# A decoder layer on one core: fourteen gate/up tiles of the first feed-forward half put in pairs with seven block products for eight

## The chip, the cores and the metric

The program runs on one core of one Trainium2 chip. The time is that of one execution on the device in microseconds (us), as a median of several runs. A separate execution is recorded by the hardware profiler, and every duration of a single instruction comes from that one. The engines are PE (TensorE, matrix products; its weight loads are listed as PEld), DVE (VectorE), ACT (ScalarE), POOL (GpSimd) and SP (SyncE, which only issues transfers here).

## What is computed

One layer on 512 tokens of width 1024: a gated feed-forward half, a mixing part (dilated attention and a diagonal state model side by side), and a second gated feed-forward half.

```python
x = x + 0.5 * rms_norm(swiglu(rms_norm(x, ffn1_pre_g), ffn1_w_in, ffn1_w_out), ffn1_post_g)
h = rms_norm(x, mix_pre_g)
q, k, v, u = split(h @ w_mix_in)
a = dilated_attention(q, k, v)
s = s5_mixer(u, a_re, a_im, log_dt, b_re, b_im, c_re, c_im, d_skip, w_glu, b_glu)
x = x + rms_norm(concat([a, s]) @ w_mix_out, mix_post_g)
x = x + 0.5 * rms_norm(swiglu(rms_norm(x, ffn2_pre_g), ffn2_w_in, ffn2_w_out), ffn2_post_g)

def swiglu(x, w_in, w_out):          # w_in: 1024 x 5632, w_out: 2816 x 1024
    gate, up = split(x @ w_in)
    return (silu(gate) * up) @ w_out
```

All is float32. The change is in the first `swiglu`, and in the point of time at which `s5_mixer`'s parameters (powers of the state factor, the matrices that go in and out of the states) are worked out.

## The kernel before, in words

**Precision.** Each float32 factor is cut in a high part in the type fp32r (ACT, a cast) and a low part (the difference, on DVE or POOL). A product is three matmuls: high x high, high x low, low x high (`mm3`). `load` fetches a weight block to a `wraw` buffer (3 of them) and cuts it to `whi` and `wlo` (4 of each); its argument `pool` puts the subtraction on POOL, otherwise it is on DVE.

**Layout.** Activations stand with features on the 128 partitions and the 512 tokens along the free dimension. Big buffers of 8 x 512 columns come from one pool of six (`b16`): `x`, `xh`, `xl`, `y`, `ah`, `al` in the first half.

**First half, `ffn` (L371).** The 2816 hidden features are 22 tiles of 128. For each tile f, `products(f)` (L388) makes gate and up, each 8 blocks x 3 matmuls of 512 columns; `hidden(f)` (L396) scales by the norm factor `r`, takes silu(gate) x up and cuts the result to `ah`, `al`, in a ring of 8 slots. Output products (`outp`, L404) are made in three parts, each over all 8 output blocks m: over tiles 0 to 6 after tile 7, over 7 to 13 after tile 14, and over 14 to 17 after tile 21 (`FMAIN`). The first writes `y`, the others add to it. The last four tiles (18 to 21) are left to `boundary` (L261), which multiplies them with the tail weights `tw` in two halves of tokens, so that the norm behind them can begin early; `load_tail` fetches those weights during tiles 18 to 21.

**The state model's parameters, `ssm_params` (L726).** A generator that `ffn` resumes between matmuls (`hook`, `step`); 35 resumptions run it to its end. In order: loads; exponentials and sines of columns of 16 on DVE; powers `pw`; four pairs of complex products (128 x 256, DVE) whose results ACT copies to two large zeroed tiles `gb`; eight groups of transposes `w1t` on PE, each copied by ACT and written to memory (`w1d`); products `kb` in two parts and transposes `kc` on PE, with `kd` written; four more complex products, copied by ACT to `zb` (two tiles in the place of `gb`, zeroed by POOL) and written as `w2d`. All its tiles lie in pools that are closed when it has ended (`early`).

The steps stand at blocks k = 5 of each gate product and k = 1 and 5 of each up product from tile 2's up product on (L385).

**Second half, `swiglu_half` (L455).** Tiles 0 to 5 are made as in the first half. Tiles 6 to 21 are made in pairs, `pair` (L550). The 1024 input features are cut in two halves and the 512 tokens in two halves, gate and up are the two rows of blocks of the weights: a 2 x 2 by 2 x 2 product, which takes seven block products of weight sums with input sums in place of eight (the scheme of Strassen and Winograd). `sums` (L514) makes the sums of the inputs, scaled by gain and norm factor, once; `plain` (L530) cuts the four plain blocks; a pair makes its own sums of weights. A block product (`times`, L554) is 24 matmuls of 256 columns: two tiles x 4 blocks x 3.

**What sets the order.** A planner places the instructions on each engine by the program's order as priority and by readiness in its own model of time; those passed through `fix`, matmuls among them, keep the program's order. Each engine then works off its list in that fixed order, and the transfers issued by SP are one list too. Buffers of a ring are reused when their last reader has ended; a pool opened in the place of a closed one waits for the last use of what lay there.

Of the kernel before, what the change touches and what calls it, by code (L numbers as in the profile page):

```python
# [8 lines left out]
F32 = mybir.dt.float32  # L9
F32R = mybir.dt.float32r  # L10
I32 = mybir.dt.int32
AF = mybir.ActivationFunctionType
# [5 lines left out]
P = 128  # L18
S = 512
# [4 lines left out]
FMAIN = ((0, 7), (7, 7), (14, 4))  # L24
# [4 lines left out]
NSTD = 6  # L29
# [14 lines left out]
class Layer:  # L44
# [326 lines left out]
    def ffn(self, n, first, scope):  # L371
# [13 lines left out]
        other = ({5: step}, {1: step, 5: step})  # L385
        between = {(nfirst, 0): {}, (nfirst, 1): {6: lambda: late[0](fixp=self.fix)}, (nfirst + 1, 0): {6: late[1]}}

        def products(f):  # L388
            o[f] = []
            for i, c in enumerate((f, NF + f)):  # L390
                w = self.ahead.pop(0) if self.ahead else self.load(w_in[c], (KD, P), pool=i == 1)
                b = self.bank("gu")
                self.mmk(b, w, self.xh, self.xl, hooks=between.get((f, i), other[i]))
                o[f].append(b)
# [9 lines left out]
        def outp(i):  # L404
            f0, nf = FMAIN[i]
            for m in range(KD):
                wh, wl = self.load(w_out[m][:, f0:f0 + nf, :].rearrange("p k m -> p (k m)"), (nf, P), pool=m % 2 == 1)
                b = self.bank("yo")
                for k in range(nf):
                    s = (f0 + k) % RING  # L410
                    self.mm3(b, wh[:, k], wl[:, k], ah(s), al(s), k == 0, k == nf - 1)
                if i == 0:
                    nc.scalar.copy(out=y(m), in_=b)
                else:
                    nc.vector.tensor_tensor(out=y(m), in0=b, in1=y(m), op=ALU.add)

        for f in range(NF):
            if f >= nfirst:
                products(f)
            if f == lag:  # L420
                for i in range(lag):
                    hidden(i)
            if f >= lag:
                hidden(f)
            if f in (7, 14):
                outp(f // 7 - 1)
            if f == NF - NT:
                for _ in hook:
                    pass
                early.close()  # L430
                tp = scope.enter_context(self.tc.tile_pool(name="bd" + n, bufs=1))
            if f >= NF - NT:
                self.load_tail(tp, w_tail, f - (NF - NT), f % 2 == 1)
        tail = lambda k: (ah((NF - NT + k) % RING), al((NF - NT + k) % RING))
        outp(2)
# [19 lines left out]
    def swiglu_half(self, first, scope):  # L455
# [4 lines left out]
        nc, V, fx = self.nc, self.nc.vector, self.fix  # L460
# [43 lines left out]
        def wsum():  # L504
            return fin.tile([P, 1024], F32, name="wsum", tag="wsum", bufs=3)

        tq = [[fin.tile([P, 1024], F32R, name="tq", tag=f"tq{q}{i}") for i in range(2)] for q in range(3)]

        def quarter(t, i, j):
            return t.pair(slice(4 * i, 4 * i + 4))[:, :, j * HT:(j + 1) * HT]  # L510

        v4 = lambda t: t.rearrange("p (k c) -> p k c", c=HT)

        def sums():  # L514
            for k in range(KD):
                V.scalar_tensor_tensor(out=self.x(k), in0=self.x(k), scalar=self.g(4, k), in1=r, op0=ALU.mult, op1=ALU.mult)
            b = lambda i, j: quarter(self.x, i, j)
            n1, n2 = wsum(), wsum()
            V.tensor_tensor(out=v4(n1), in0=b(0, 0), in1=b(0, 1), op=ALU.subtract)
            V.scalar_tensor_tensor(out=v4(n2), in0=v4(n1), scalar=-1.0, in1=b(1, 1), op0=ALU.mult, op1=ALU.subtract)  # L520
            self.split(*tq[0], n2)
            t = wsum()
            V.scalar_tensor_tensor(out=v4(t), in0=v4(n2), scalar=-1.0, in1=b(1, 0), op0=ALU.mult, op1=ALU.subtract)
            self.split(*tq[2], t)
            t = wsum()
            V.tensor_tensor(out=v4(t), in0=b(1, 1), in1=b(0, 1), op=ALU.subtract)
            self.split(*tq[1], t)
            return n1

        def plain(n1):  # L530
            bh, bl = self.b16("bh", F32R), self.b16("bl", F32R)
            v = lambda t, q: t.rearrange("p (q k) c -> p q (k c)", q=4)[:, q]
            src = [quarter(self.x, 0, 0), quarter(self.x, 1, 0), quarter(self.x, 1, 1), v4(n1)]
            for q, s in enumerate(src):
                self.split(v4(v(bh, q)), v4(v(bl, q)), s)
            return [(v(bh, q), v(bl, q)) for q in range(4)]

        def block(f, up, kh, extra):
            t = (fin.tile([P, 1024], F32, name="wx", tag="wx", bufs=3) if extra else
                 self.wp.tile([P, 1024], F32, name="wraw", tag="wraw", bufs=3))  # L540
            src = w_in[f + NF * up:f + NF * up + 2, :, kh * S:(kh + 1) * S].rearrange("f p c -> p f c")
            nc.sync.dma_start(out=t.rearrange("p (f c) -> p f c", f=2), in_=src)
            return t

        def cut(t, pool=False):
            hi, lo = (self.wp.tile([P, 1024], F32R, name=n, tag=n, bufs=4) for n in ("whi", "wlo"))
            self.wsplit(t, hi, lo, pool)
            return hi, lo

        def pair(f, b11, b21, b22, n1, n2, t3, t4):  # L550
            add = lambda x, z, t: V.tensor_tensor(out=t, in0=x, in1=z, op=ALU.add)
            X = self.bank("wx")

            def times(bank, w, xb, first):  # L554
                for g in range(2):
                    for k in range(4):
                        c, m = slice(k * HT, (k + 1) * HT), slice((4 * g + k) * P, (4 * g + k + 1) * P)
                        st = first and g == 0 and k == 0
                        for i, (wi, xi) in enumerate(((0, 0), (0, 1), (1, 0))):
                            self.mm(bank[:, g * HT:(g + 1) * HT], lhsT=w[wi][:, m], rhs=xb[xi][:, c],  # L560
                                    start=st and i == 0, stop=g == 1 and k == 3 and i == 2, skip_group_check=True)

            def keep(bank):
                t = self.tmp("kp")
                nc.scalar.copy(out=t, in_=bank)
                return t

            p2 = lambda t: t.rearrange("p (f c) -> p f c", f=2)
            gt = fin.tile([P, 2, S], F32, name="gp", tag="gp", bufs=2)
            half = lambda t, h: t[:, :, h * HT:(h + 1) * HT]  # L570
            a11 = block(f, 0, 0, False)
            h11 = cut(a11)
            times(X, h11, b11, True)
            s1 = keep(X)
            a12 = block(f, 0, 1, False)
            h12 = cut(a12, True)
            Y = self.bank("wy")
            times(Y, h12, b21, True)
            V.tensor_tensor(out=half(gt, 0), in0=p2(Y), in1=p2(s1), op=ALU.add)
            a21, a22 = block(f, 1, 0, True), block(f, 1, 1, True)  # L580
            c3 = wsum()
            add(a11, a21, c3)
            c2 = wsum()
            add(c3, a22, c2)
            times(X, cut(c2), n2, False)
            s2 = keep(X)
            c1 = wsum()
            add(a21, a22, c1)
            Q = self.bank("wq")
            times(Q, cut(c1), n1, True)  # L590
            q = keep(Q)
            times(X, cut(c3), t3, False)
            V.tensor_tensor(out=q, in0=X, in1=q, op=ALU.add)
            add(c2, a12, c2)
            times(Q, cut(c2), b22, False)
            V.tensor_tensor(out=half(gt, 1), in0=p2(Q), in1=p2(s2), op=ALU.add)
            nc.scalar.activation(out=gt, in_=gt, func=AF.Silu)
            times(X, cut(a22, True), t4, False)
            s = f % RING
            dst = lambda t, h: half(t.pair(slice(s, s + 2)), h)  # L600
            for h, u in ((1, q), (0, X)):
                V.scalar_tensor_tensor(out=half(gt, h), in0=p2(u), scalar=-1.0, in1=half(gt, h), op0=ALU.mult, op1=ALU.mult)
                if f == NF - 2:
                    self.split(dst(ah, h), dst(al, h), half(gt, h))
            if f < NF - 2:
                self.split(ah.pair(slice(s, s + 2)), al.pair(slice(s, s + 2)), gt)

        for f in range(NSTD):
# [7 lines left out]
            if f == 3:  # L616
                for _ in hook:
                    pass
                n1 = sums()
        blocks = plain(n1)  # L620
# [3 lines left out]
        for f in range(NSTD, NF, 2):  # L624
            pair(f, *blocks, *tq)
            if f in (10, 16):
                outp(f // 6)
# [781 lines left out]
```

## Time and profile before

| | us |
|---|---|
| median of 3 runs | 941.23 |
| lowest and highest | 939.71 and 943.09 |
| the profiled execution | 939.08 |
| its span, first to last instruction | 937.3 |
| first half: tile 0 to the end of the third output product | 8.9 to 353.8 |
| second half: start of the first output product to the end of the last pair | 649.9 to 908.1 |

A row of the chain of waits or of the timeline gives start, length, engine or what, the line of the code, what is written and read, and the count (x24). L132 is the helper through which every matmul goes, so there the tile's name tells them apart: `gu` is a gate or up product, `yo` an output product, `yt` the tail's, `wx`, `wy`, `wq` the block products of a pair. A group's row ends with busy time, mean ns of one, and the idle time before with what ended it. A row of a view by stretches gives, for each engine, busy us and in brackets the number of instructions. "before" in square brackets means that the engine stood idle for that long.

### The profile page before, as it was taken

How to read it: one execution, taken by the hardware profiler on the slowest of the kernel's cores; microseconds unless marked ns; L12 is line 12 of the kernel's file. 1: busy time of each engine (PE TensorE's matmuls, PEld its weight loads, DVE VectorE, ACT ScalarE, POOL GpSimd, SP SyncE). 2: the span in 40 equal slices, each digit the busy share in tenths (PEclk: the TensorE clock that was granted, in tenths of full speed). 3: DMA queues.
4: the chain of work that ended last, by engine and by line, in shares of the span. 5: the costliest groups of instructions: out<-in, count | busy, mean ns of one | idle time of the engine just before them, and what ended most of it. 6: DMA issues, size and time to landing. Idle time of an engine off the chain costs nothing.

```text
span 937.3 us, 14181 instructions
## 1 busy us (share of the span) xinstructions
PE 925.7 (99%) x5658; PEld 803.6 (86%) x5658; DVE 588.5 (63%) x994; ACT 407.3 (43%) x650; POOL 225.0 (24%) x134
## 2 busy tenths in 40 slices
PE   8999999999999999999999999999999999999996
PEld 6888888888888889978777889988899989998995
DVE  6999214464246544947989467679357547745856
ACT  7354324452233322526637564465255414541542
POOL 0234222232223222420000024521222212221321
PEclk9999999999999999999999999999999999999999
DMA  8223333353334232086221452243323322332222
GB/s 272 90 93 118 105 106 124 131 180 101 113 107 144 75 123 69 24 236 174 87 83 57 136 180 92 75 150 113 113 91 111 116 90 90 113 113 91 92 90 90
DMA packets 44001, 106.74 MB, mean 114 GB/s; under 512 B 7808, under 2 KB 11136, under 8 KB 43392
## 3 DMA queue, kind: packets, MB, share of 16 engines
q1 hardware_dynamic: 42352, 102.21, 33.4%
q10 hardware_dynamic: 1584, 3.63, 1.1%
q8 instruction: 44, 0.72, 0.3%
q14 instruction: 21, 0.17, 0.1%
HBM read 96.13 MB, written 9.70 MB: 113 GB/s over the span
## 4 chain that ended last, share of the span: by engine, by line
PE 94%; DVE 3%; ACT 1%; issue 1%; DMA 0%; SPq 0%; POOLq 0%; POOL 0%; DVEq 0%; ACTq 0%
PE gu L132 29%; PE yo L132 21%; PE wx L132 10%; PE yt L132 6%; PE first L132 6%; PE wq L132 5%; PE prj L132 4%; PE wy L132 2%; PE prv L132 2%; PE mo L132 2%; PE st L132 1%; PE ys L132 1%; PE gl L132 1%; PE pt L999 1%; PE sc L132 1%
## 5 line engine op out<-in xcount | busy, mean ns | idle before, releaser
L107 POOL TENSOR_TENSOR wlo<-wraw,whi 128x1024 fp32r<-128x1024 f32 (+2 forms) x55 | 139.0, 2528 | 402.4 <-ACT whi L105 388.5
L105 ACT CAST whi<-wraw 128x1024 fp32r<-128x1024 f32 (+5 forms) x143 | 139.9, 985 | 213.5 <-PE yo L132 87.7
L107 DVE TENSOR_TENSOR wlo<-wraw,whi 128x1024 fp32r<-128x1024 f32 (+5 forms) x88 | 110.7, 1265 | 104.8 <-ACT whi L105 104.5
L132 PE MATMUL gu<-xh,whi 128*128 128x512 f32 x400 | 158.0, 395 | 0.0
L132 PE MATMUL gu<-xh,wlo 128*128 128x512 f32 x400 | 156.2, 390 | 0.1
L132 PE MATMUL gu<-xl,whi 128*128 128x512 f32 x400 | 155.7, 389 | 0.0
L132 PEld LDWEIGHTS gu<-xh,wlo 128*128 128x128 f32 x400 | 75.1, 188 | 16.4 <-DVE wlo L107 0.6
L132 PEld LDWEIGHTS gu<-xh,whi 128*128 128x128 f32 x400 | 75.1, 188 | 15.3 <-issue 0.4
L132 PEld LDWEIGHTS gu<-xl,whi 128*128 128x128 f32 x400 | 75.2, 188 | 15.1
L132 PE MATMUL wx<-tq,whi 128*128 128x256 f32 x384 | 69.0, 280 | 0.0
L107 DVE TENSOR_TENSOR wlo<-wsum,whi 128x1024 fp32r<-128x1024 f32 x32 | 39.1, 1221 | 35.2 <-ACT whi L105 35.2
L132 PEld LDWEIGHTS wx<-tq,whi 128*128 128x128 f32 x384 | 58.8, 188 | 0.0
L132 PE MATMUL yo<-whi,ah 128*128 128x512 f32 x144 | 56.1, 389 | 0.0
L132 PE MATMUL yo<-whi,al 128*128 128x512 f32 x144 | 56.0, 389 | 0.0
L132 PE MATMUL yo<-ah,whi 128*128 128x512 f32 x144 | 56.0, 389 | 0.0
L132 PE MATMUL yo<-al,whi 128*128 128x512 f32 x144 | 56.0, 389 | 0.0
L132 PE MATMUL yo<-ah,wlo 128*128 128x512 f32 x144 | 56.0, 389 | 0.0
L132 PE MATMUL yo<-wlo,ah 128*128 128x512 f32 x144 | 56.0, 389 | 0.0
L105 ACT CAST whi<-wsum 128x1024 fp32r<-128x1024 f32 x32 | 33.6, 1049 | 49.6 <-PE yo L132 21.9
L132 PE MATMUL wx<-tq,wlo 128*128 128x256 f32 x192 | 53.6, 279 | 0.0
L152 DVE TENSOR_TENSOR al<-ut,ah 128x512 fp32r<-128x512 f32 x28 | 36.1, 1293 | 13.8 <-ACT ah L151 13.7
L132 PE MATMUL first<-xh,whi 128*128 128x256 f32 (+1 forms) x144 | 43.2, 300 | 0.8 <-ACT xh L154 0.8
(258 smaller groups left out, 2084.0 us busy)
## 6 DMA issues: line engine op xcount, KB each, us to landing
wraw<-w1i SPq DMA_DIRECT2D x42, 512.0 KB, 3.5
wraw<-w2i SPq DMA_DIRECT2D x28, 512.0 KB, 3.7
wraw<-w2o SPq DMA_DIRECT2D x18, 512.0 KB, 4.0
wx<-w2i SPq DMA_DIRECT2D x16, 512.0 KB, 3.7
wraw<-w1o SPq DMA_DIRECT2D x16, 448.0 KB, 3.3
wraw<-wmi SPq DMA_DIRECT2D x12, 512.0 KB, 3.6
x<-xT SPq DMA_DIRECT2D x8, 256.0 KB, 4.5
w1d<-w1s SPq DMA_DIRECT2D x8, 256.0 KB, 2.9
```

The costliest lines, as they stand in the source:

```text
L105: fix(self.nc.scalar.copy(out=hi, in_=raw))
L107: fix(eng.tensor_tensor(out=lo, in0=raw, in1=hi.bitcast(F32), op=ALU.subtract))
L132: i = self.nc.tensor.matmul(*a, **k)
L152: fix(nc.vector.tensor_tensor(out=lo, in0=src, in1=hi.bitcast(F32), op=ALU.subtract))
L999: self.fix(nc.tensor.transpose(b[i][:, o:o + P], sc[:, c:c + P], self.ident))
```

## The change

- Tiles 0 to 7 of the first half are made one by one as before, tiles 8 to 21 in seven pairs. `sums`, `plain` and `pair` become one function `seven` for both halves, with these differences: the scaled inputs are written to four buffers of their own (three `wx`, one `gp`) and not over `x`, in 16 scalings of 256 columns and not 8 of 512, since the first half still needs `x`. The blocks of the up weights use the three `wx` buffers. `pair` has an argument `late`: whether the result is cut by token halves; in the first half it is not.
- `FMAIN` becomes tiles 0 to 7, 8 to 13, 14 to 17. The first output product is made in two parts: output blocks 0 to 3 right behind tile 7; then the parameters' pools are closed, a pool `fin` for the pairs is opened in their place, `sums` and `plain` are issued; then output blocks 4 to 7. The second part of the output comes after the pair 12, 13.
- The steps of `ssm_params` stand at k = 1, 3, 5 of gate and up, and at every second tile of the first four blocks of the first output product.
- The tail weights are loaded inside the third output product, one ahead of each of its blocks 3 to 6, after the pairs' pool is closed. In that product, block 1's subtraction is on DVE and not on POOL.

```diff
-FMAIN = ((0, 7), (7, 7), (14, 4))
+FMAIN = ((0, 8), (8, 6), (14, 4))
-NSTD = 6
+NSTD = (8, 6)
@@ ffn
-        other = ({5: step}, {1: step, 5: step})
+        other = {1: step, 3: step, 5: step}
...
-                self.mmk(b, w, self.xh, self.xl, hooks=between.get((f, i), other[i]))
+                self.mmk(b, w, self.xh, self.xl, hooks=between.get((f, i), other))
...
-        def outp(i):
+        def outp(i, ms=range(KD), tails=None):
             f0, nf = FMAIN[i]
-            for m in range(KD):
-                wh, wl = self.load(w_out[m][:, f0:f0 + nf, :].rearrange("p k m -> p (k m)"), (nf, P), pool=m % 2 == 1)
+            for m in ms:
+                if tails and 2 < m < 3 + NT:
+                    self.load_tail(tails, w_tail, m - 3, m % 2 == 1)
+                wh, wl = self.load(w_out[m][:, f0:f0 + nf, :].rearrange("p k m -> p (k m)"), (nf, P), pool=m % 2 == 1 and (i < 2 or m > 2))
                 b = self.bank("yo")
                 for k in range(nf):
                     s = (f0 + k) % RING
                     self.mm3(b, wh[:, k], wl[:, k], ah(s), al(s), k == 0, k == nf - 1)
+                    if i == 0 and m < 4 and k % 2:
+                        step()
...
-        for f in range(NF):
+        for f in range(NSTD[0]):
...
-            if f in (7, 14):
-                outp(f // 7 - 1)
-            if f == NF - NT:
-                for _ in hook:
-                    pass
-                early.close()
-                tp = scope.enter_context(self.tc.tile_pool(name="bd" + n, bufs=1))
-            if f >= NF - NT:
-                self.load_tail(tp, w_tail, f - (NF - NT), f % 2 == 1)
+        outp(0, range(4))
+        for _ in hook:
+            pass
+        early.close()
+        with ExitStack() as mid:
+            fin = mid.enter_context(self.tc.tile_pool(name="fin" + n, bufs=1))
+            sums, plain, pair = self.seven(fin, w_in, 0, r, ah, al)
+            sums()
+            plain()
+            outp(0, range(4, KD))
+            for f in range(NSTD[0], NF, 2):
+                pair(f)
+                if f == 12:
+                    outp(1)
+        tp = scope.enter_context(self.tc.tile_pool(name="bd" + n, bufs=1))
         tail = lambda k: (ah((NF - NT + k) % RING), al((NF - NT + k) % RING))
-        outp(2)
+        outp(2, tails=tp)
@@ seven: the new form of sums, and what differs in pair
+        wx = lambda: fin.tile([P, 1024], F32, name="wx", tag="wx", bufs=3)
+        gp = lambda: fin.tile([P, 1024], F32, name="gp", tag="gp", bufs=2)
...
+            q = [[wx(), gp()], [wx(), wx()]]
             for k in range(KD):
-                V.scalar_tensor_tensor(out=self.x(k), in0=self.x(k), scalar=self.g(4, k), in1=r, op0=ALU.mult, op1=ALU.mult)
+                for j in range(2):
+                    c = slice(j * HT, (j + 1) * HT)
+                    V.scalar_tensor_tensor(out=v4(q[k // 4][j])[:, k % 4], in0=self.x(k)[:, c], scalar=self.g(ig, k),
+                                           in1=r[:, c], op0=ALU.mult, op1=ALU.mult)
...
-                if f == NF - 2:
+                if late:
                     self.split(dst(ah, h), dst(al, h), half(gt, h))
-            if f < NF - 2:
+            if not late:
                 self.split(ah.pair(slice(s, s + 2)), al.pair(slice(s, s + 2)), gt)
```

The rest of `seven` (n1, n2 and the two further sums cut to `tq`, the cuts of the plain blocks, the seven block products of a pair in their order) is as in `swiglu_half` before.

More of the change, by code (lines that the diff above doesn't have):

```diff
@@ L455, in swiglu_half @@
     def swiglu_half(self, first, scope):
-        nc, V, fx = self.nc, self.nc.vector, self.fix
+        nc, V = self.nc, self.nc.vector
         w_in, w_out, w_tail = (self.a["w2" + t] for t in "iot")
@@ L502, in outp @@
                         V.tensor_tensor(out=y(b, d), in0=b4[b], in1=y(b, d), op=ALU.add)
[L504 to L515, printed above, removed]
-                V.scalar_tensor_tensor(out=self.x(k), in0=self.x(k), scalar=self.g(4, k), in1=r, op0=ALU.mult, op1=ALU.mult)
[L517 to L602, printed above, removed]
-                if f == NF - 2:
-                    self.split(dst(ah, h), dst(al, h), half(gt, h))
-            if f < NF - 2:
-                self.split(ah.pair(slice(s, s + 2)), al.pair(slice(s, s + 2)), gt)
@@ L608, in swiglu_half @@
-        for f in range(NSTD):
+        sums, plain, pair = self.seven(fin, w_in, 4, r, ah, al)
+        for f in range(NSTD[1]):
             if f >= len(o0) // 2:
@@ L618, in swiglu_half @@
                     pass
-                n1 = sums()
-        blocks = plain(n1)
+                sums()
+        plain()
         yk = self.ktiles("y")
@@ L623, in swiglu_half @@
         outp(0)
-        for f in range(NSTD, NF, 2):
-            pair(f, *blocks, *tq)
+        for f in range(NSTD[1], NF, 2):
+            pair(f, f == NF - 2)
             if f in (10, 16):
```

88 lines of the change are left out of this document (added).

## The prediction

> **What bounds the kernel now.** I read the page first (busy time and the shares of the chain that ended last), then that chain in order of time, then busy time by stage.
>
> ```profile
> span 937.3 us, 14181 instructions
> ```
>
> ```profile
> PE 925.7 (99%) x5658; PEld 803.6 (86%) x5658; DVE 588.5 (63%) x994; ACT 407.3 (43%) x650; POOL 225.0 (24%) x134
> ```
>
> ```profile
> PE 94%; DVE 3%; ACT 1%; issue 1%; DMA 0%; SPq 0%; POOLq 0%; POOL 0%; DVEq 0%; ACTq 0%
> ```
>
> TensorE (PE) carries 94% of the chain. Busy PE alone proves little, since the ends of matmuls are modelled; the chain says more, because at each step it names what was waited for. In the first half it is PE alone:
>
> ```profile
> 96.76 38.08 PE yo L132 x168
> 134.84 9.52 PE gu L132 x42
> ...
> 217.84 38.08 PE yo L132 x168
> 255.93 76.16 PE gu L132 x336
> 332.08 21.76 PE yo L132 x96
> ```
>
> Columns: start, length, what, matmuls. Gate/up tiles 15 to 21 are 336 matmuls in 76.16 us with nothing between them: 0.2267 us for one of 512 columns, 5.44 for a block row of 24, 10.88 for a tile. Tiles 8 to 14, as many, run from 134.84 to 217.84: 83.00 us. The 6.84 us above 76.16 are PE work for the state model's parameters (w1t, kb, kc) between them. So this half gets shorter by what PE is spared, and longer where another engine comes late.
>
> The second half has the other form already, tiles in pairs with seven block products. By stage:
>
> ```profile
> 20.00:97.00 77.00, 76.98 (x348) 63.72 (x347) 70.50 (x198) 34.01 (x54) 26.15 (x10) 1.00 0.33 109
> 97.00:135.00 38.00, 38.00 (x169) 31.46 (x169) 7.66 (x7) 11.79 (x17) 9.26 (x4) 1.00 0.34 110
> ...
> 682.57:742.62 60.05, 60.05 (x506) 60.05 (x505) 38.68 (x39) 31.72 (x37) 15.06 (x6) 1.00 0.30 100
> ```
>
> Columns: stretch, length, then busy us of PE, weight loads, DVE, ACT, POOL, then granted clock, DMA share, GB/s. Three pairs take 60.05 us, PE without a gap, DVE busy 38.68. From 20 to 97 us, ahead of the first output product, DVE is busy 70.50 of 77.00: the stretch with little room, and the change moves work into it. In the 38 us after it DVE does 7.66.
>
> **The change part by part.**
>
> *Pairs.* Two tiles cost 2 x 10.88 = 21.76 us. A pair costs 60.05 / 3 = 20.02: 168 matmuls of 256 columns at 0.119 us. The arithmetic falls by 1/8, but 0.119 is more than half of 0.2267, so 8% is left. Seven pairs for fourteen tiles: 7 x 1.74 = **12.2 us less on PE**. The pairs of the second half have the same loads, sums, splits and banks and keep PE full, so I add nothing inside a pair. PE has no gap in this half to win back, so no term below goes under nothing.
>
> *Output products.* 8 + 6 + 4 tiles are as many matmuls as 7 + 7 + 4, and the parameters' 6.84 us move ahead: nothing on PE from either.
>
> [...]
>
> *Parameters sooner.* The generator has 35 steps. They came at three per tile and ended in tile 13; now they come at six per tile, 33 of them in tiles 2 to 7 and two in the first output product. By the parameters' own tiles, DVE's share is early already:
>
> ```profile
> 20.00:97.00 77.00, 0.00 (x0) 0.00 (x0) 32.63 (x153) 6.46 (x16) 0.00 (x0) 1.00 0.33 109
> 135.00:218.00 83.00, 2.16 (x64) 1.62 (x64) 4.23 (x10) 7.92 (x20) 0.98 (x2) 1.00 0.43 139
> ```
>
> DVE did 32.63 us of it before 97, as fill; only 4.23 move ahead. The stretch itself grows by the 6.84 of PE work, so DVE then has 70.50 + 4.23 = 74.7 of 83.8 us: full to 89%, against 92% before. ACT goes from 34 to about 50. One clash counts:
>
> ```profile
> 35.10 2.39 DVE L741 TENSOR_TENSOR pp<-pp 128x16 f32<-128x16 f32 x1
> ```
>
> ```profile
> 62.89 0.69 DVE L401 TENSOR_TENSOR ut<-ut,gt 128x512 f32<-128x512 f32 x1
> ```
>
> ```profile
> 80.53 3.42 DVE L107 TENSOR_TENSOR wlo<-wraw,whi 128x1024 fp32r<-128x1024 f32 x1
> ```
>
> ```profile
> 34.93 2.53 POOL L107 TENSOR_TENSOR wlo<-wraw,whi 128x1024 fp32r<-128x1024 f32 x1
> ```
>
> ```profile
> 60.71 3.56 POOL L873 MEMSET gb<- 128x2048 f32 x2
> ```
>
> A DVE operation of 16 columns takes 2.39 us beside a POOL subtraction; one of 512 takes its plain 0.69 beside POOL's memsets. [...] By the rows, the two memsets that move ahead cost DVE nothing (3.6 us if they blocked it), and POOL's reading subtractions are as many as before. The last wlo of the stretch is done at 83.95, tile 7 begins at 96.76 - 10.88 = 85.88: 1.9 us of room. The first transpose w1t now stands at tile 5, up, k = 3, about 64.1 + 5.4 + 2.7 = 72.2 us, and needs copies that were done at 72.4:
>
> ```profile
> 68.15 4.25 ACT L883 COPY gb<-pp 64x256 f32<-64x256 f32 x10
> ```
>
> Their sources now rank ahead of tiles 4 and 5's own work. Stalls here are bounded by 0 and, if DVE comes 5 us later, some 3 (5 less 1.9); I take 0.3, as nothing is added to DVE that the stretch doesn't get back.
>
> *Tile 7 into the first output product.* Tile 7 is now its eighth term; before, it was not in it. Its end, where tile 7's products stopped at 96.76:
>
> ```profile
> 96.80 0.69 DVE L400 TENSOR_TENSOR ut<-gu,rs 128x512 f32<-128x512 f32 x1 [2.20 <-PE gu L132]
> ```
>
> ```profile
> 98.97 1.84 DVE L152 TENSOR_TENSOR al<-ut,ah 128x512 fp32r<-128x512 f32 x1 [0.69 <-ACT ah L151]
> ```
>
> al is there 4.05 us after the last matmul; PE wants it at 7 x 0.68 + 0.23 = 4.99. So 0.9 us of room, but ACT's copies into zb and DVE's last products (2.6 us per step) now fall there. Bounds 0 and 3.5; I take 0.8.
>
> *Handover of memory.* The pairs' 14 buffers take the place of the parameters', so the sums wait for the last use of those:
>
> ```profile
> 188.45 3.56 POOL L931 MEMSET zb<- 128x2048 f32 x2 [1.18 <-PE kb L132]
> ```
>
> ```profile
> 192.30 5.62 ACT L942 COPY zb<-pp 64x256 f32<-64x256 f32 x14
> ```
>
> ```profile
> 197.14 1.17 SPq L944 DMA_DIRECT2D w2d<-zb  x2
> ```
>
> ```profile
> w2d<-zb SPq DMA_DIRECT2D x2, 1024.0 KB, 4.9
> ```
>
> POOL begins 188.45, the write is issued by 198.3 and lands 4.9 later: 14.8 us after kb. With T the end of tile 7's products (about 96.8 + 6.8 = 103.6), kb ends at T - 7.2 (ten steps of 0.68 and kc follow), so the buffers are free at T + 7.6. Then DVE's sums, priced from the second half:
>
> ```profile
> L305 DVE SCALAR_TENSOR_TENSOR ymix<-ymix,sm,rp 128x256 f32<-128x256 f32 x16 | 7.2, 470 | 0.0
> ```
>
> ```profile
> L152 DVE TENSOR_TENSOR bl<-x,bh 128x1024 fp32r<-128x1024 f32 x3 | 3.7, 1218 | 0.0
> ```
>
> ```profile
> L152 DVE TENSOR_TENSOR tq<-wsum,tq 128x1024 fp32r<-128x1024 f32 x3 | 3.6, 1214 | 0.0
> ```
>
> 16 scalings of 256 columns x 0.47, four sums of 1024 x 1.22 and seven low halves x 1.22: 20.9 us, with two weight subtractions 23.3. All is ready at T + 31; PE reaches the first pair at T + 64 x 0.68 = T + 43.5. So it is hidden, with 12.5 us to spare. ACT's seven casts of 1024 run beside, and the up blocks of the first pair, which reuse two of those buffers, load within that room:
>
> ```profile
> L105 ACT CAST whi<-wraw 128x1024 fp32r<-128x1024 f32 x112 | 117.2, 1052 | 155.7 <-PE yo L132 67.2 <-issue 18.5 <-PE gu L132 15.1
> ```
>
> ```profile
> wx<-w2i SPq DMA_DIRECT2D x16, 512.0 KB, 3.7
> ```
>
> On SP the two parameter writes stand among weight loads, which at one per 5.44 us have room for 3.
>
> *Pair 12 into the second output product.* In the second half, four tiles lie ahead of the fresh pair at four matmul groups each; here its two tiles are terms 5 and 6, at T' + 2.72 us, the low half wanted at T' + 2.95. Where pairs ended at 702.59 and 742.62:
>
> ```profile
> 705.49 1.23 DVE L152 TENSOR_TENSOR al<-gp,ah 128x1024 fp32r<-128x1024 f32 x1
> ```
>
> ```profile
> 744.81 1.22 DVE L152 TENSOR_TENSOR al<-gp,ah 128x1024 fp32r<-128x1024 f32 x1
> ```
>
> It is there 4.1 and 3.4 us after: a stall of 0.5 to 1.2, new. I take 0.7.
>
> *Tail weights.* The four loads that stood in tiles 18 to 21 now lie inside the third output product, 21.76 us, beside its own eight. Three raw buffers turn over in about 7 us (a transfer, a cast, a subtraction):
>
> ```profile
> wraw<-w1t SPq DMA_DIRECT2D x4, 512.0 KB, 3.5
> ```
>
> ```profile
> wraw<-w1o SPq DMA_DIRECT2D x8, 256.0 KB, 2.6
> ```
>
> ```profile
> L107 POOL TENSOR_TENSOR tw<-wraw,tw 128x1024 fp32r<-128x1024 f32 x3 | 7.8, 2596 | 25.9 <-ACT tw L105 25.9
> ```
>
> ```profile
> L105 ACT CAST whi<-wraw 128x512 fp32r<-128x512 f32 x8 | 5.0, 621 | 16.6 <-PE gu L132 10.6 <-PE yo L132 4.2 <-issue 1.7
> ```
>
> ```profile
> L107 POOL TENSOR_TENSOR wlo<-wraw,whi 128x512 fp32r<-128x512 f32 x4 | 5.2, 1289 | 26.0 <-ACT whi L105 26.0
> ```
>
> A tail load holds one for 3.5 + 1.05 + 1.2 or 2.6, an output load for 2.6 + 0.6 + 0.7 or 1.3; the four tails and the five output loads that can't be fetched ahead make about 47 buffer-us, 16 on three buffers, under 21.76. Followed load by load, in the order in which they are written, output loads 5 and 6 come some 0.6 late. Bounds 0 and 4; I take 0.7.
>
> **Sum:** -12.2 + 0.3 + 0.8 + 0.7 + 0.7 = **-9.7 us**. The profiled execution took 939.08 (span 937.3); the median of the three runs is 941.23, 2.1 above. On the median: **931.5 us**. About 0.3% (2.8 us) is what a measurement of this kernel can tell from no change.
>
> **The rivals.**
>
> (1) Forecast, the pairs' gain less short stalls: 928 to 934, **0.66**. For it: 60.05 us of gapless pairs.
>
> (2) The crowded stretch starves PE: DVE, ACT or the w1s writes come 3 to 9 us later than reckoned, and wlo, w1t or tile 7 make PE wait. For it: 1.9 and 0.9 us of room. Against it: the same DVE fill, and idle DVE behind it. 941.2 - 9.7 + 3 to 9 = 934.5 to 940.5, **0.18**, two thirds of it below 938.4 and the rest within 0.3%.
>
> (3) Slower: the buffers' handover comes too late. DVE keeps its order, so a first sum that waits holds up the weight subtractions behind it. It costs from release at T + 20 on (43.5 less 23.3), and turns the gain into more than 2.8 us of loss from T + 33 on, 40 us after kb where 14.8 are reckoned. At T + 45: 941.2 - 9.7 + 25 = 956. Against it: that chain is measured. **0.05**.
>
> (4) The change doesn't do what it says: weight loads bind and a pair of 168 loads waits for each load's 188 ns. 7 x (31.6 - 21.76) = 69 us more, 1010. Against it: in the gapless pairs weight loads were busy 60.05 of 60.05 at 0.119 spacing. [...] **0.01**.
>
> ```profile
> L132 PEld LDWEIGHTS wx<-tq,whi 128*128 128x128 f32 x384 | 58.8, 188 | 0.0
> ```
>
> (5) All four joins fit and the median falls a little low: 926 to 928, **0.10**.
>
> **How the numbers follow.** Faster by over 0.3%: 0.66 + 0.10 + two thirds of 0.18, 0.88; within: 0.06; slower: 0.06. The range 927 to 938 holds (1), half of (5) and over half of (2), and leaves out 0.19.
>
> **What would show it.** Right: seven stretches of 168 matmuls in 20.0 us each between the first and the third output product; no PE wait over 1 us ahead of tile 7; a wait of 0.5 to 1.2 on al inside the second output product. Wrong: PE waits on wlo or gb in tiles 5 to 7; the first pair waiting on tq, bh or wx; waits on whi in the third output product of more than 2 us; first products of the next boundary late for tw.

## The result and the profile after

| | before | after |
|---|---|---|
| median, us | 941.23 (5 runs) | 936.23 (5 runs) |
| lowest and highest | 939.71, 943.09 | 933.38, 936.75 |
| ratio, 95% interval | | 0.9937 (0.9915 to 0.996) |
| the profiled execution, its span | 939.08, 937.3 | 936.74, 935.0 |

The kernel is about 5.5 us faster (5.0 by the medians, 5.9 by the ratio). In a second series it gave 934.47 and 0.9946. The forecast was 931.5: the sign is right, the time lies in the range, and nearly half of the 9.7 us is missing. The profiled executions show still less, 2.3 us between the spans, so their rows can say where it went.

The page after, busy time and the shares of the chain that ended last:

```profile
span 935.0 us, 15349 instructions
...
PE 916.7 (98%) x6162; PEld 818.3 (88%) x6162; DVE 649.0 (69%) x1065; ACT 442.8 (47%) x685; POOL 226.8 (24%) x133
...
PE 80%; DVE 10%; DMA 4%; ACT 3%; issue 2%; POOL 1%; SPq 0%; POOLq 0%; DVEq 0%; ACTq 0%
```

PE is busy 9.0 us less. Its share of the chain falls from 94% to 80%, but that is no measure of its waiting: the chain up to 112.76 runs through DVE, ACT and transfers, beside a PE that is busy nearly all the while, and a second profile of this kernel (`changed_again`) has 90%. What PE waited for stands below. By stage (columns as before: stretch, length, PE, weight loads, DVE, ACT, POOL, granted clock, DMA share, GB/s):

```profile
105.19:153.21 48.02, 45.88 (x195) 37.26 (x194) 36.47 (x42) 22.63 (x33) 13.23 (x4) 0.96 0.47 163
153.21:213.26 60.05, 60.05 (x505) 60.05 (x505) 38.33 (x39) 31.04 (x37) 14.53 (x6) 1.00 0.29 95
247.10:327.19 80.09, 80.09 (x674) 80.09 (x673) 53.92 (x56) 40.65 (x48) 18.16 (x7) 1.00 0.23 74
```

The second and third rows are the seven pairs: 140.14 us without a gap in PE, 20.02 each, where fourteen tiles took 14 x 10.88 = 152.32. So the 12.2 us are there in full. The first row is the first output product, from its first matmul, right behind tile 7's products, to the first pair: 64 x 0.68 = 43.5 us of work that took 48.02, at a mean clock of 0.96. What PE waited for (engine, waited for, us in total, times, longest):

```profile
PE yo L132 <- DVE al L152: 2.9, 2, 2.0
...
PE kc L939 <- ACT kt L935: 1.2, 1, 1.2
PE yo L132 <- POOL wlo L107: 1.1, 1, 1.1
...
PE gu L132 <- DVE wlo L107: 0.7, 1, 0.7
```

None of these four stands in the same list of before. From the starts of the matmuls (distance to the next one less the matmul's own 0.227) come their places and whole lengths:

| where | us | lost |
|---|---|---|
| `kc` on `kt`, before the first output product | 98.99 | 1.36 |
| tile 7's term in its first block, on `ah` and `al` | 109.72 | 0.29 + 2.29 |
| eight matmuls behind it at 0.427 us | 113.78 to 117.19 | 1.6 |
| pair 12's term in the second output product, on `al` | 215.85 | 1.03 |
| block 5 of the third output product, on `wlo` | 340.88 | 1.23 |
| second half, first product behind the norm, on `wlo` | 599.10 | 0.90, before 0.25 |

The third row is no wait. The view by stretches around it:

```profile
108.00:113.78 5.78, 3.64 (x15) 2.46 (x14) 2.48 (x1) 2.64 (x5) 2.35 (x1) 1.00 0.91 363
113.78:117.19 3.41, 3.41 (x9) 2.63 (x8) 2.82 (x6) 1.04 (x2) 0.00 (x0) 0.50 0.62 190
117.19:121.00 3.81, 3.81 (x18) 3.15 (x17) 3.81 (x10) 0.58 (x1) 0.00 (x0) 1.00 0.28 110
```

PE waits for tile 7, and then runs at half clock for 3.41 us; "busy 3.41 of 3.41" hides it, the count (9 for some 15) and the clock column show it. Ahead of it stand 2.58 us of waiting (the last section has more on it).

The five rows up to 350 us make 7.8 us, and 12.2 - 7.8 = 4.4; the tail's first product starts at 350.38 where it was 353.84, 3.5 ahead, so that 0.9 us lie in pieces too small to follow. The second half gives back 0.65 more. A wait of `yt` on `so` in the mixing part takes most of the rest; it is 1.52 here, and 0.49 in before and in the second profile of this same kernel, so that it differs from one execution to the next.

**Why `kt` and `al` are late** (`wlo` follows under `tails_dve`). The timeline of DVE, of POOL and of ACT after, around tile 7 (start, length, engine, line, what, idle before):

```profile
96.75 2.64 DVE L401 TENSOR_TENSOR ut<-ut,gt 128x512 f32<-128x512 f32 x1
...
104.25 1.76 DVE L756 TENSOR_TENSOR pp<-pp,pp 128x256 f32<-128x256 f32 x5
106.11 0.42 DVE L758 SCALAR_TENSOR_TENSOR pp<-pp,pp 128x256 f32<-128x256 f32 x1
106.45 0.68 DVE L400 TENSOR_TENSOR ut<-gu,rs 128x512 f32<-128x512 f32 x1
107.24 0.69 DVE L401 TENSOR_TENSOR ut<-ut,gt 128x512 f32<-128x512 f32 x1
110.22 2.48 DVE L152 TENSOR_TENSOR al<-ut,ah 128x512 fp32r<-128x512 f32 x1 [2.29 <-ACT ah L151]
```

```profile
96.44 2.40 POOL L107 TENSOR_TENSOR wlo<-wraw,whi 128x1024 fp32r<-128x1024 f32 x1 [8.95 <-ACT whi L105]
98.78 3.56 POOL L946 MEMSET zb<- 128x2048 f32 x2
109.80 2.35 POOL L107 TENSOR_TENSOR wlo<-wraw,whi 128x1024 fp32r<-128x1024 f32 x1 [7.46 <-ACT whi L105]
```

```profile
99.42 0.62 ACT L151 CAST ah<-ut 128x512 fp32r<-128x512 f32 x1 [3.11 <-DVE ut L401]
99.95 0.58 ACT L935 COPY kt<-kb 128x512 f32<-128x512 f32 x1
100.42 1.06 ACT L105 CAST whi<-wraw 128x1024 fp32r<-128x1024 f32 x1
101.38 3.34 ACT L957 COPY zb<-pp 64x256 f32<-64x256 f32 x8
104.74 0.63 ACT L399 ACTIVATE gt<-gt 128x512 f32<-128x512 f32 x1
105.28 3.32 ACT L957 COPY zb<-pp 64x256 f32<-64x256 f32 x8
108.62 1.05 ACT L105 CAST whi<-wraw 128x1024 fp32r<-128x1024 f32 x1
109.57 0.61 ACT L151 CAST ah<-ut 128x512 fp32r<-128x512 f32 x1
```

The first output matmul starts at 105.19. Tile 7's `ut` starts 1.3 us later, behind the parameters' last products; its `ah` starts 1.6 us after `ut` is done, behind eight copies into `zb` and the cast of output weights; and its `al` takes 2.48 us beside POOL's cut of output block 3, where tile 6's took 0.69 (at 100.07). It is done 7.5 us after that first matmul started, where PE wanted it after 4.99. The `kc` wait comes from the same list of ACT: tile 6's `ut` takes 2.64 beside POOL's cut of block 1 (tile 7's takes 0.69), and ACT works in order, `ah` and then `kt`. From tile 6's `ah` at 99.42 to tile 7's at 109.57 ACT has no pause, so what came late at tile 6 is still late at tile 7.

### The profile page after: what moved, and what is told of

Same layout as the page of the kernel before. It is cut to its first block, busy times and chain, and to the rows that moved or that the text cites. A ratio compares the mean times of both kernels' runs of the same rounds, so it can differ in the third digit from the quotient of the medians.

```text
span 935.0 us, 15349 instructions
## 1 busy us (share of the span) xinstructions
PE 916.7 (98%) x6162; PEld 818.3 (88%) x6162; DVE 649.0 (69%) x1065; ACT 442.8 (47%) x685; POOL 226.8 (24%) x133
## 4 chain that ended last, share of the span: by engine, by line
PE 80%; DVE 10%; DMA 4%; ACT 3%; issue 2%; POOL 1%; SPq 0%; POOLq 0%; DVEq 0%; ACTq 0%
PE yo L132 19%; PE wx L132 18%; PE wq L132 9%; PE yt L132 6%; PE gu L132 5%; PE first L132 5%; PE wy L132 5%; PE prj L132 4%; PE prv L132 2%; DVE pp L756 2%; PE mo L132 2%; DVE wlo L107 1%; PE st L132 1%; PE ys L132 1%; DVE al L152 1%
## 5 line engine op out<-in xcount | busy, mean ns | idle before, releaser
L132 PE MATMUL wx<-tq,whi 128*128 128x256 f32 x720 | 129.3, 280 | 0.0
L132 PEld LDWEIGHTS wx<-tq,whi 128*128 128x128 f32 x720 | 110.3, 188 | 0.0
L132 PE MATMUL wx<-tq,wlo 128*128 128x256 f32 x360 | 100.4, 279 | 0.0
L132 PE MATMUL gu<-xh,whi 128*128 128x512 f32 x176 | 70.8, 402 | 0.0
L132 PE MATMUL gu<-xh,wlo 128*128 128x512 f32 x176 | 68.9, 391 | 0.7 <-DVE wlo L107 0.7
L132 PE MATMUL gu<-xl,whi 128*128 128x512 f32 x176 | 68.7, 390 | 0.0
L132 PE MATMUL wq<-bh,wlo 128*128 128x256 f32 x240 | 68.1, 284 | 0.0
L132 PE MATMUL wq<-bh,whi 128*128 128x256 f32 x240 | 68.0, 283 | 0.0
L132 PE MATMUL wq<-bl,whi 128*128 128x256 f32 x240 | 67.9, 283 | 0.0
L132 PEld LDWEIGHTS wx<-tq,wlo 128*128 128x128 f32 x360 | 67.6, 188 | 0.0
```

The source lines that it names most:

```text
L132: i = self.nc.tensor.matmul(*a, **k)
```

## The experiments

Ratios are to the kernel before, run on the same chip in the same series. Two theories stood at the start. **Mine**: the pairs bring 12.2 us, and the waits at tile 7, `kc`, pair 12 and the tail weights, with the half clock, take about half of it. **Rival**: the pairs themselves bring only some 5 us in time that counts, and the waits cover idle time that is there anyway.

**The pairs alone undone** (`singles`): tiles 8 to 21 one by one, everything else as in the change.

```diff
-            sums, plain, pair = self.seven(fin, w_in, 0, r, ah, al)
...
-            for f in range(NSTD[0], NF, 2):
-                pair(f)
-                if f == 12:
-                    outp(1)
+        for f in range(NSTD[0], NF):
+            products(f)
+            hidden(f)
+            if f == 14:
+                outp(1)
```

> Tiles 8 to 21 one by one again, without the sums of inputs; all else as in the change (parameters sooner, output products by 8, 6 and 4, tail weights in the third; the second output product after tile 14). Theory 1 (the pairs gave their whole 12.2 us on PE and the joins around them took about 8.7 back): slower than the changed kernel by 12.2 less the wait at pair 12 (1.2), so about 947, some 6 us above the kernel before. Rival (the pairs themselves gain less in the first half, 5 us, and the joins cost little): about 941, no slower than the kernel before.

Measured 944.7, ratio 1.004 (1.0024 to 1.0056): slower than the kernel before. Against the mean 0.9942 of the change's two series, the pairs and their own waits bring 0.0098 x 940 = 9.2 us, which by the two intervals is good to about 2 us. This kernel has no wait for pair 12 and none for the tail weights; 12.2 less their 1.2 and 1.4 (with the matmuls lost around them) is 9.6. The rival's 5 us fall. The rest of the change alone costs 3.8 us, about what the waits at `kc` (1.40) and tile 7 (2.59 in its profile) come to.

**The parameters' steps alone** (`steps_sooner`): the kernel before with six steps a tile.

```diff
-        other = ({5: step}, {1: step, 5: step})
+        other = {1: step, 3: step, 5: step}
```

> The kernel before with the parameters' steps at k = 1, 3, 5 of gate and up and nothing else of the change: products by 7, 7, 4, no pairs. Theory 1 (the crowding as such costs only the wait of kc for kt, 1.4 us; the dear wait at tile 7 comes from tile 7 being a term of the first output product): 1.4 us more than the kernel before, ratio 1.0015, no PE gap over 0.5 us but that at kc, clock 1.00. Rival (the crowded stretch starves PE by itself): gaps of 3 us and more between 60 and 110 us, ratio over 1.003.

Measured 940.19, ratio 1.0004 (0.9993 to 1.0014). Its one new wait is `kc` on `kt`, 0.57 us. The crowded stretch by itself costs nothing that can be measured. Tile 7's `al` is late here too, 6.6 us after the first output matmul started (4.2 in before), but this first output product does not take tile 7, and nobody waits. The stretch hurts where tile 7 is wanted at once behind it.

**Tile 7 wanted later** (`tile7_last`): output blocks 0 and 1 are first made over tiles 0 to 6, and both take tile 7 after that, 4.76 us later than before.

```diff
-                for k in range(nf):
+            n = nf - len(wait)
+            head = list(ms)[:2] if wait else []
+            for m in head:
+                fetch(m)
+                terms(m, range(n))
+            for m in head:
+                terms(m, range(n, nf))
...
-        outp(0, range(4))
+        outp(0, range(4), wait=(7,))
```

> In the first output product the terms of tile 7 for output blocks 0 and 1 come after the other seven terms of both: 4.8 us more room for tile 7's low half. Theory 1 (the wait of 2.6 us there also brings the half clock of the 3.2 us behind it): both go, granted clock 1.00 from 108 to 122 us, 4.4 us less than the changed kernel, about 931.8. Rival A (the half clock has another cause): it stays, 2.6 us less, about 933.6. Rival B (DVE is behind as a whole): the wait comes back at the next weight block, no gain.

Measured 932.8, ratio 0.9916 (0.9901 to 0.9931). The stretch that held the wait, in this kernel:

```profile
108.00:113.78 5.78, 5.78 (x27) 4.80 (x26) 2.53 (x1) 1.80 (x3) 2.40 (x1) 1.00 0.98 376
```

PE full, clock 1.00; `al` is as late as ever (DVE's one operation still takes 2.53 beside POOL's 2.40), and nobody waits for it. That gives back 2.4 us against 0.9942, good to about 2 us. The trace of the change had 2.58 of wait and 1.6 of slow matmuls. That less than these 4.2 comes back is within the intervals; and not each execution of the change has the half clock (last section), while this kernel has a new wait of 0.41 us at 137.70.

**Tile 7 later still to be had** (`al7_later`): the change, with `al` of tile 7 written three times more, with the same values, behind its own write.

```diff
+            for _ in range(3 if f == 7 else 0):
+                nc.vector.tensor_tensor(out=al(7), in0=ut, in1=ah(7).bitcast(F32), op=ALU.subtract)
```

> Tile 7's low half is written four times over, 3 x 0.69 us more on DVE with the POOL subtraction beside it. The first write's end releases nothing sooner, so PE waits about 2.1 us longer (4.7 in all). Theory 1 (clock falls for a window behind a long enough wait): the half clock stays one window of about 3.3 us or becomes two; 2.1 to 3.8 us more than the changed kernel, 938.3 to 940. Rival (the clock has nothing to do with the wait): 2.1 more and the half clock at the same place as before.

Measured 938.89, ratio 0.998 (0.9971 to 0.999). The wait grew from 2.29 to 4.47 and the half clock from 3.41 to 6.83 us:

```profile
113.34:120.17 6.83, 4.84 (x11) 3.80 (x12) 4.80 (x9) 1.53 (x2) 0.00 (x0) 0.50 0.46 140
```

Of these 6.83 us, 1.99 lie in the wait itself, where the clock costs nothing. The matmuls behind it lose 2.4 us where those of the change lose 1.6. So the traces show 2.2 us more of wait and 0.8 more lost to the clock, 3.0 together; the ratio is 0.0038 above 0.9942, 3.6 us, good to about 1.6. In these two traces a us of wait at this place costs more than a us; the times alone are too coarse to show it.

**POOL's cut of output block 1 moved to DVE** (`block1_dve`). It was meant to take the POOL cut from beside `al`; but the edit moves block 1 alone, and the cut beside `al` is block 3's, which stays on POOL.

```diff
-pool=m % 2 == 1 and (i < 2 or m > 2))
+pool=m % 2 == 1 and (i == 1 or m > 2))
```

> In the first output product the low half of the odd weight blocks is cut on DVE instead of POOL. Theory 1 (DVE's subtraction for tile 7 took 2.48 us because a POOL subtraction ran beside it, 0.69 alone): the low half is there 1.8 us sooner if DVE is free, the wait falls from 2.6 to about 0.8 us, and if a wait that short doesn't lower the clock, 3.6 us are saved: about 932.6. Rival A (a wait of 0.8 lowers the clock too): 1.8 saved, about 934.4. Rival B (the weight cut that is now on DVE goes ahead of tile 7's subtraction): no gain or a loss of 1.

Measured 933.86, ratio 0.9922 (0.9904 to 0.9939); the wait at `kc` is gone. DVE's and POOL's timelines of this kernel:

```profile
96.49 0.69 DVE L401 TENSOR_TENSOR ut<-ut,gt 128x512 f32<-128x512 f32 x1
...
108.01 2.49 DVE L152 TENSOR_TENSOR al<-ut,ah 128x512 fp32r<-128x512 f32 x1 [2.29 <-ACT ah L151]
```

```profile
107.59 2.36 POOL L107 TENSOR_TENSOR wlo<-wraw,whi 128x1024 fp32r<-128x1024 f32 x1 [7.99 <-ACT whi L105]
```

The POOL cut at 96.4, which had held `ut` up, was block 1's: without it `ut` takes 0.69 and the `kc` wait is gone. At 107.6 POOL cuts block 3's weights as in the change, so `al` still takes 2.49 and PE waits 2.04, with the half clock behind it. The run shows the cause of the `kc` wait, and that tile 6 sets part of tile 7's delay: the two waits were 1.36 + 2.58 = 3.94 us in the change's profile and are 2.04 here, 1.90 less, about what `ut` got shorter (1.95). The ratio is 1.9 us under 0.9942, within the intervals. What the clash of `al` with block 3's cut costs was not isolated.

**`kc` one resumption later** (`kc_later`).

```diff
         nc.scalar.copy(out=kt, in_=kb)
         yield
+        yield
```

> One resumption more between the copy kt and the transposes kc: two blocks of products (1.36 us) stand between them now. Theory 1 (kc waits 1.4 us for kt, because ACT's high half of tile 6 ahead of it waits for a DVE product slowed by POOL): the wait at 99 us goes but the waits of tile 7 keep their size, since DVE and ACT run from PE's products: 1.3 us less than the changed kernel. Rival (what PE wins there it waits again at tile 7, whose low half hangs on DVE's and ACT's own backlog): no gain, the wait at 110 us grows from 2.6 to 3.9.

Measured 936.75, ratio 0.9961 (0.9949 to 0.9974): nothing won. The 1.36 us at `kc` are gone, and the list of waits shows where they went:

```profile
PE yo L132 <- DVE al L152: 2.9, 2, 2.0
PE yo L132 <- ACT ah L151: 1.3, 1, 1.3
```

PE reaches tile 7's term that much sooner and now waits for `ah` too, 1.42 us. The wait at `kc` was no cost of its own; tile 7 sets the time there.

**Pair 12 wanted later** (`pair12_last`): the edit of `tile7_last` in the second output product instead, for its terms 5 and 6.

```diff
-                    outp(1)
+                    outp(1, wait=(4, 5))
```

> In the second output product the terms of tiles 12 and 13 for output blocks 0 and 1 come after the other four of both: 2.7 us more room. Theory 1: the wait of 1.03 us on the low half of the fresh pair goes, 1.2 us less than the changed kernel. Rival (the next weight blocks come late instead, as two weight blocks are held at once): no gain.

Measured 935.06, ratio 0.9939 (0.9922 to 0.9956). The wait of 1.03 us is gone from the trace; a us alone can't be told from 0.9942 with these intervals.

**Tail weights cut on DVE** (`tails_dve`).

```diff
-                    self.load_tail(tails, w_tail, m - 3, m % 2 == 1)
+                    self.load_tail(tails, w_tail, m - 3, False)
```

> The low halves of all four tail weight blocks are cut on DVE and none on POOL. Theory 1 (output block 5 waits 1.2 us for its POOL cut, which stands behind a tail cut of 2.4 us): that wait goes, a smaller one of up to 0.3 on block 6's transfer stays: about 1.1 us less than the changed kernel. Rival (three raw buffers are what is short): the wait moves to block 6, no gain.

Measured 934.7, ratio 0.9943 (0.9923 to 0.9963), the same. The wait of 1.23 us is gone from the trace. In the change POOL had done the tail's cut first:

```profile
338.64 2.41 POOL L107 TENSOR_TENSOR tw<-wraw,tw 128x1024 fp32r<-128x1024 f32 x1 [4.75 <-ACT tw L105]
341.00 1.27 POOL L107 TENSOR_TENSOR wlo<-wraw,whi 128x512 fp32r<-128x512 f32 x1
```

`whi` of block 5 had been cast by 339.76; `wlo` began 1.2 us later, when POOL was free. So this wait was for POOL and not for a raw buffer.

**All four** (`joined`): `tile7_last`, `kc_later`, `pair12_last` and `tails_dve` in one kernel.

```diff
-                    self.load_tail(tails, w_tail, m - 3, m % 2 == 1)
+                    self.load_tail(tails, w_tail, m - 3, False)
...
-        outp(0, range(4))
+        outp(0, range(4), wait=(7,))
...
-                    outp(1)
+                    outp(1, wait=(4, 5))
...
         nc.scalar.copy(out=kt, in_=kb)
         yield
+        yield
```

> The edits of tile7_last, kc_later, pair12_last and tails_dve together. Theory 1 (four joins, each with its own cause, 4.4 + 1.4 + 1.2 + 1.1 us of the 12.2): the waits in the first half fall under 1.5 us in all, the time to the kernel before is 11 us less, ratio 0.988. Rival (the waits have one cause, the crowded DVE, and move on): not better than tile7_last alone, ratio 0.9916.

Measured 929.26, ratio 0.9883 (0.9865 to 0.99): 11.0 us faster than before, 5.5 faster than the change by the ratios. Its chain, in order of time:

```profile
136.83 10.97 PE yo L132 x46
147.79 2.87 PE wx L132 x24
...
320.59 22.33 PE yo L132 x96
342.92 15.55 PE yt L132 x132
```

The first pair starts at 147.79 (after: 153.21; by the prediction's steps 103.6 + 43.5 = 147.1), and the tail's products at 342.92, 10.9 ahead of before. Three of the four gave nothing measurable alone; `kc`'s us stays won only where tile 7 has room.

**The second half's scalings as before** (`joined_half2`): `joined`, with `x` scaled in place in the second half (8 operations of 512 columns for 16 of 256).

```diff
+            if ig == 4:
+                for k in range(KD):
+                    V.scalar_tensor_tensor(out=self.x(k), in0=self.x(k), scalar=self.g(ig, k), in1=r, op0=ALU.mult, op1=ALU.mult)
+                q = [[self.x.pair(slice(4 * i, 4 * i + 4))[:, :, j * HT:(j + 1) * HT] for j in range(2)] for i in range(2)]
```

> The kernel called joined, and in the second half the scaled inputs written over x again, in 8 scalings of 512 columns as in the kernel before. Theory 1 (in the second half the scalings of 256 columns to buffers of their own are placed ahead of a weight cut on DVE, and PE waits 0.95 us there at about 590 us where it waited 0.25): that wait is 0.25 again, 0.7 us less than joined, ratio 0.9875. Rival (that wait has another cause): ratio 0.9883 as joined.

Measured 928.92, ratio 0.9883 (0.987 to 0.9895). The wait at the first product behind the norm falls from 0.96 to 0.25 us in the traces; the time does not show it. In the change, DVE had put a scaling ahead of that product's weights (chain of after, then of before):

```profile
598.45 0.47 DVE wx L483
598.92 1.15 DVE wlo L107
```

```profile
599.78 1.06 ACT whi L105
600.86 1.24 DVE wlo L107
```

**The change once more** (`changed_again`), without an edit.

> The changed kernel once more, on the chip of the other kernels of this call. Ratio to the kernel before 0.994. If the half clock depends on where the wait falls in a window that runs on its own, its times fall in two groups about 1.8 us apart, the shorter with the granted clock of the kernel before (0.998), the longer 0.002 lower; if it doesn't, all show the lower clock.

Measured 934.47 (932.49 to 937.58), ratio 0.9946 (0.9931 to 0.9961). The six times (932.49, 933.41, 933.79, 935.14, 936.54, 937.58) do not part into two groups, and the mean granted clock of a run can't sort them: it counts also the half clock at the end, 2.0 us in the profile of after and 4.2 in that of before, where PE has no matmul left. In its profile the same waits, 2.58 us at tile 7, but no half clock:

```profile
108.00:113.78 5.78, 3.63 (x15) 2.44 (x15) 2.49 (x1) 2.65 (x4) 2.35 (x1) 1.00 0.97 373
113.78:117.19 3.41, 3.41 (x17) 2.81 (x16) 3.12 (x6) 0.75 (x2) 0.00 (x0) 1.00 0.60 187
```

## Why the prediction was right, and where it was not

The time lies in the range, but not in the band that the forecast itself was given: (1) says 928 to 934, and 936.2 lies in that of rival (2), 934.5 to 940.5. What (2) describes did happen, at one of its three places: DVE and ACT brought tile 7 later than reckoned, and PE waited for it; for `wlo` and `w1t` it did not wait there. The range reaches up to 938 because of (2), so that it held the time in spite of the sum, which is luck for the sum.

- **Pairs, -12.2.** Right to the tenth, in the trace (140.14 us for seven) and, less its own waits, on the clock (`singles`, 9.2, give or take 2, where 9.6 were due). Weight loads don't bind: three pairs take 60.05 us here too, with PE busy throughout. Rival (4) falls.
- **Tile 7 into the first output product, +0.8.** This step failed. Its mechanism was named: ACT's copies into `zb` and DVE's last products fall there. But the price was taken near the low end of 0 to 3.5, and the wait was 2.58. Counted from the start of the first output matmul, `al` came after 7.5 us, where it took 4.2 in before (the prediction's 4.05 counts from the modelled end of the last product, 0.16 later). `ut` began 1.1 later than in before, `ah` 1.6 later behind `ut`, and `al` took 0.6 longer: 3.3 together, of which 0.8 was room. Followed along DVE's and ACT's lists, the two delays could have been seen: a step of 2.6 us of DVE products and 3.3 us of copies lie across. The prediction let tile 7's low half hang on the end of tile 7's products; `kc_later` shows that it hangs on ACT's and DVE's own lists too, since there PE came sooner and waited longer. The half clock behind the wait, 1.6 us more in some executions, was in no term and not within the bounds.
- **Crowded stretch, +0.3.** Too small, in another place than thought: not `w1t` or `wlo`, but `kc`, 1.36 us. Yet it is no separate loss (`kc_later`), since tile 7 would have taken it. That the stretch starves PE even where tile 7 is not wanted at once is refuted by `steps_sooner`; rival (2) is left with tile 7.
- **Handover of memory, 0.** Right in effect: the first pair waits for nothing. The row of the last sum's low half:

```profile
141.52 1.22 DVE L152 TENSOR_TENSOR tq<-wsum,tq 128x1024 fp32r<-128x1024 f32 x1
```

  It ends at 142.74, 37.6 after the first output matmul started, where 31 behind tile 7's products was reckoned: 6.6 of the 12.5 us of room were used. Rival (3) falls.
- **Pair 12, +0.7.** 1.03 of wait, inside 0.5 to 1.2. Here too `al` lay beside a POOL cut, 1.90 for 1.23.
- **Tail weights, +0.7.** 1.23, at block 5 as followed, but through POOL's order and not through the raw buffers.
- **Second half, no term.** 0.65 in the trace: the shared `seven` doubles the number of scalings, and one of them gets ahead of the weights for a waiting product.

By the terms: the waits were put at 2.5 us and came to 1.36 + 2.58 + 1.03 + 1.23 + 0.65 = 6.9, with 1.6 for the clock in some executions. 12.2 - 6.9 = 5.3, or 3.7 with the half clock; measured were 5.0 to 5.9. The sum is of one profile, and the rest of the program differs from one execution to the next by as much as the two figures do (the wait of `yt`, 1.52 or 0.49).

## What to carry to other kernels

When a tile's result is moved next to its first use, follow its last operations on each engine's list one by one, with what is already queued there, and price DVE operations like `ut` and `al` by whether a POOL subtraction lies beside them (0.69 us without, 2.48 and 2.64 with it, here). Where a fresh result is one term of a sum over blocks, take that term last in the first two blocks: the work stays the same and the wait had room to vanish. Removing one wait on a chain with a later wait only moves it; edits like `kc_later` must be tried together with the one that makes room behind them.

## What the runs showed of the hardware beside this

**The clock after a wait.** In after the granted clock changes at 113.78, 117.19 and 932.98 us. The half clock between the first two lasts 3.413 us and the full clock behind it 815.785, 239 times that; the full clock ahead lasts 109.226, 32 times, and the one in the profile of before 928.425, 272 times. So in these two profiles the changes lie whole multiples of 3.413 us apart. PE's wait at tile 7's term and the half clock behind it, in six profiles with that wait:

| kernel | wait | half clock from | for | waited in the 3.41 us ahead of it |
|---|---|---|---|---|
| after | 2.58 | 113.78 | 3.41 | 2.29 |
| `block1_dve` | 2.04 | 111.9 | 3.4 | 2.04 |
| `kc_later` | 1.42 + 2.28 | 111.0 | 6.8 | 2.76 |
| `al7_later` | 0.29 + 4.47 | 113.34 | 6.83 | 2.77 |
| `changed_again` | 2.58 | none | | |
| `singles` | 2.59 | none | | |

After and `changed_again` have the same wait, and in the second the clock stays. So the length of the wait alone does not decide it. What else does, such as the window in the expectation of `changed_again`, was not shown: no run moved the wait in time on purpose. The waits of 1.36, 1.03 and 1.23 us in after (`kc`, pair 12, tail weights) brought none. Where the wait went on into the half clock, by 0.95 us in `kc_later` and 1.99 in `al7_later`, this lasted 6.8 us, twice 3.41. In after PE runs at full clock for 1.02 us behind the wait (112.76 to 113.78) and only then slows down.

The half clock costs 1.6 us in the change's profile. It can be only a part of the spread of the times: the change took 932.49 to 937.58 in its six runs of the second series, and the kernel before, which has no such wait, 938.48 to 942.32 in seventeen.

**A POOL subtraction beside a row of DVE operations.** The prediction priced only what POOL's subtractions cost DVE. In `tile7_last` POOL's subtraction, which took 2.40 us at 109.44 in the same profile, and DVE's operations at its end:

```profile
129.41 14.54 POOL L107 TENSOR_TENSOR wlo<-wraw,whi 128x1024 fp32r<-128x1024 f32 x1 [8.65 <-ACT whi L105]
```

```profile
138.21 1.21 DVE L152 TENSOR_TENSOR tq<-wsum,tq 128x1024 fp32r<-128x1024 f32 x1
139.35 1.21 DVE L107 TENSOR_TENSOR wlo<-wraw,whi 128x1024 fp32r<-128x1024 f32 x1
140.48 1.21 DVE L550 TENSOR_TENSOR wsum<-wraw,wx 128x1024 f32<-128x1024 f32 x1
141.73 3.30 DVE L550 TENSOR_TENSOR wsum<-wsum,wx 128x1024 f32<-128x1024 f32 x1
144.96 1.21 DVE L550 TENSOR_TENSOR wsum<-wx 128x1024 f32<-128x1024 f32 x1
```

DVE's operations follow each other every 1.13 us at a length of 1.21, without a gap from 125.72 on: each starts before the one ahead has ended. The first with a gap ahead of it (0.04 us, at 141.73) takes 3.30, and POOL ends at 143.95, 2.2 after that gap. So POOL's 14.54 can be read as some 12 us of waiting for a train of DVE operations and 2.4 of work; this is an estimate from these rows, and no run took the train away. PE had other blocks to do meanwhile; the 0.41 us that it lost at 137.70 were a wait for a cut on DVE.
